# Branch products of a hybrid encoder block: where the tanh pool lies, how early weights are asked for, and at which units the next branch's operands are loaded

## The chip, the core and the metric

The kernel runs on one core of a Trainium2 chip. A core has a matrix engine (PE, with its weight loads shown apart as PEld), three engines for elementwise work (DVE, ACT and POOL) and SP, whose queue issues most of the transfers. Each engine works through its own instructions in order and waits on semaphores where a result of another engine, or a landed transfer, is needed. PE reads its operands from SBUF and writes to PSUM. The metric is the time of one execution on the device in microseconds (us); lower is better.

## The reference, cut to what matters

One encoder block: three mixers (dilated window attention, grouped attention, cross-attention into a memory) give `oa`, `ob` and `om` of 1024 tokens by 512 channels. Each is multiplied by a gate path and projected to 1024 channels; the three products are added under sigmoid gates, and one more projection follows.

```python
ya = (oa * jax.nn.silu(ga)) @ w_br_a[layer]
yb = (ob * jax.nn.silu(gb)) @ w_br_b[layer]
ym = (om * jax.nn.silu(gm)) @ w_br_m[layer]
gates = jax.nn.sigmoid((mg + b_merge[layer]).astype(jnp.float32)).astype(dt).reshape(b, s, N_BRANCHES, d)
merged = gates[:, :, 0] * ya + gates[:, :, 1] * yb + gates[:, :, 2] * ym
out = merged @ w_out[layer]
x = x + rms_norm(out, g_post[layer])
```

The last three lines of gates and products, and `merged`, are the stage that the change edits.

## The kernel before, in words

Everything is computed channels by tokens, in float32 by splitting each operand into a high part in the PE's own format (`hh`, `wh`) and the rest (`hl`, `wl`): a product is three matmul passes, high by high, high by low and low by high. `split` (L104) makes the two parts: ACT copies the high part (L105), DVE subtracts it (L106).

The gates are made first, as tanh, in products that save multiplications by the Strassen scheme (the loop at L1410, seven products a pair, `slot` and `evac`). Their results go to DRAM as `thd`, a tile of 128 channels by 1024 tokens for each of 3 branches and 8 channel blocks. The last ones are written from the tiles `rs` (L1283) by ACT's queue (L1288).

Then come the branch products, 24 units: `steps` (L1336) counts them with m, n is the branch in the order 2, 1, 0 of i, and f the channel block. A unit (`y_unit`, L1444) is 24 matmuls of 512 columns at L125 into a PSUM tile `sc`, of which there are three. For one unit these things are done in other places:

- `y_load(m)` (L1338) asks for its weights (`wbr`, 256 KB) into a raw tile `wr`, of which there are two, so the load for unit m waits until the raw tile of unit m - 2 has been split. `y_split(m)` (L1344) makes the two parts, in a ring of two `wh` tiles.
- `th_load(m)` (L1434) brings its tanh tile (512 KB) back from `thd`, four buffers.
- `y_evac(m)` (L1456) multiplies PSUM by (1 + tanh) on DVE: for the first branch straight into an accumulator `acc` (L1462), later into `th` (L1464), which POOL then adds to `acc` (L1465).

The operands of the next branch are prepared in the same loop, four tiles k = 0 to 3. `g_load(j, k)` (L1312) loads the attention output `ot` and the gate path (into `gt` or into `raw`), 512 KB each, both from DRAM; for branch 1 `r_load(k)` (L1319) adds two row broadcasts `raw<-rld` of 256 KB. One unit later `g_mult` (L1325) multiplies them on DVE (L1327, and L1329 for the broadcast), and one unit after that `g_split` (L1331) splits the product into `hh` and `hl`. From m = 10 on the weights of the last projection are loaded too (`wo_load`, L1440) and from m = 12 on split (DVE writes `wol`, or `hl` once that is free).

From L1237 on the order is written out by hand: ACT, DVE, POOL and SP work in the order of the program, as PE does throughout. So the order of the calls in the loop at L1479 is the order on each engine. What is issued after L1511 (the last projection with `gp`, `xt`, `res`) is placed by a scheduler.

Tiles live in pools that are stacked in SBUF. A tile that lies on a closed pool's memory waits for the last users of what lay there. In the kernel before, `mg` (the last projection's weights and the accumulators) lies at the bottom of the space that the Strassen stage leaves, and `my` (the `th` and `raw` tiles) above it, there on the `ch` and `rs` tiles. A third pool, `pre`, on the other side, has `ot` and `gt`. There are eight completion semaphores for transfers, used in turn, so a transfer also waits until the one eight places earlier has landed.

Of the kernel before, what the change touches and what calls it, by code (L numbers as in the profile page):

```python
# [15 lines left out]
S = 1024  # L16
# [34 lines left out]
def block(ctx: ExitStack, tc: tile.TileContext, x, xT, memT, cst, msk, bcst, tabA, gpost,  # L51
# [21 lines left out]
    def end_psum():  # L73
        bank["pool"].__exit__(None, None, None)
# [29 lines left out]
    def split(dst_h, dst_l, src):  # L104
        A.activation(dst_h, src, AF.Copy)  # L105
        V.tensor_tensor(dst_l, src, dst_h.bitcast(F32), op=OP.subtract)  # L106
# [128 lines left out]
    def pool(name, side="left"):  # L235
        p = tc.tile_pool(name=name, bufs=1, side=side, reuse_waits="tile")
        return p, p.__enter__()

    def close(p):
        p.__exit__(None, None, None)  # L240
# [584 lines left out]
    with tc.tile_pool(name="aa", bufs=1, reuse_waits="tile") as aa:  # L825
# [344 lines left out]
        def load_pair(n, u):  # L1170
            BL[n][u] = wp.tile([P, 1024], F32, name="wr", bufs=WR)
            nc.sync.dma_start(BL[n][u], wu[U_M + pairs[n][u]])

        def own_blocks(n):
            wh = wp.tile([P, 1024], R, name="wh")
            wl = wp.tile([P, 1024], R, name="wl")
            split(wh, wl, BL[n][0])
            for j in range(2):
                BL[n][("A11", "A12")[j]] = wh[:, half[j]], wl[:, half[j]]
# [17 lines left out]
        def split_block(nm, k):  # L1197
            h, l = TB[nm][k]
            split(h, l, l.bitcast(F32))
# [54 lines left out]
    def weight_sum(n, j):  # L1254
        u, v, op = {1: (part(n, 2), part(n, 3), OP.add), 2: (SF[0], part(n, 0), OP.subtract),
                    3: (part(n, 0), part(n, 2), OP.subtract), 4: (part(n, 1), SF[1], OP.subtract)}[j]
        G.tensor_tensor(SF[j - 1], u, v, op=op)  # L1257

    def block_of(n, nm):
        src = part(n, 3) if nm == "A22" else SF[int(nm[1]) - 1]  # L1260
        t = sr.tile([P, 2, 512], R, name="ch", bufs=5)
        split(t[:, 0], t[:, 1], src)
        BL[n][nm] = t[:, 0], t[:, 1]
# [48 lines left out]
    def g_load(i, k):  # L1312
        ot = pre["p"].tile([P, S], F32, name="ot", bufs=4)
        nc.sync.dma_start(ot, od[i, k])
        gt = my.tile([P, S], F32, name="raw", bufs=3) if i < 2 and k % 2 else pre["p"].tile([P, S], F32, name="gt", bufs=1)
        nc.sync.dma_start(gt, g2d[i, k])
        GG[i, k] = [ot, gt]

    def r_load(k):  # L1319
        rt = my.tile([P, S], F32, name="raw", bufs=3)  # L1320
        for h in range(2):
            nc.sync.dma_start(rt[h * 64:h * 64 + 64], rld[2 * k + h:2 * k + h + 1].to_broadcast([64, S]))
        GG[1, k].append(rt)

    def g_mult(i, k):  # L1325
        ot, gt = GG[i, k][:2]
        V.scalar_tensor_tensor(ot, ot, 0.5, gt, op0=OP.mult, op1=OP.mult)  # L1327
        if i == 1:
            V.tensor_tensor(ot, ot, GG[i, k][2], op=OP.mult)  # L1329

    def g_split(i, k, t):  # L1331
        b = k + 4 * (i == 1)
        split(hh[b][:, t], hl[b][:, t], GG[i, k][0][:, t])
# [4 lines left out]
    def y_load(m):  # L1338
        if m < len(steps):
            _, i, f = steps[m]  # L1340
            YW[m] = wp.tile([P, 1024], F32, name="wr", bufs=WR)
            nc.sync.dma_start(YW[m][:, 0:512], wbr[i, f])

    def y_split(m):  # L1344
        if m < len(steps):
            t = wp.tile([P, 1024], R, name="wh")
            split(t[:, 0:512], t[:, 512:1024], YW[m][:, 0:512])
            YW[m] = [t[:, 512 * x:512 * x + 512].rearrange("p (k f) -> p k f", k=4) for x in range(2)]

    pre = {}  # L1350
# [3 lines left out]
    def slot(n, i):  # L1354

        first = n == 0
        if not first and i == 1 and n < last:
            load_pair(n + 1, 1)
        if i == 6 and n + 1 < last:
            load_pair(n + 2, 0)  # L1360
        todo_ = (("S2",), ("S3", "A22"), ("S4",), ("S1",)) if first else (("A22",), ("S4",), ("S1",))
        for nm in todo_[i] if i < len(todo_) else ():
            block_of(n, nm)
        if first:
            for nm, k in {2: (("T1", 0), ("T1", 1)), 3: (("T1", 2), ("T1", 3)), 4: (("T4", 0), ("T4", 1)),
                          5: (("T4", 2), ("T4", 3))}.get(i, ()):
                split_block(nm, k)
        if n < last:
            if i == 3:
                weight_sum(n + 1, 1)  # L1370
                weight_sum(n + 1, 3)
                own_blocks(n + 1)
            elif i == 4:
                weight_sum(n + 1, 2)
                block_of(n + 1, "S3")
            elif i == 5:
                weight_sum(n + 1, 4)
                block_of(n + 1, "S2")
        if (n, i) in COM:
            com[COM[n, i]]()  # L1380
        if (n, i) == (5, 0):
            close(cbp)
            pre["pp"], pre["p"] = pool("pre", "right")
        k = n - (last - 4)
        if 0 <= k < 4:
            if i == 0:
                g_load(2, k)
            elif i == 4:
                g_mult(2, k)
        if n == last:  # L1390
            if i == 0:
                y_load(0)
                y_load(1)
            elif i in (3, 4):
                for k in range(2 * i - 6, 2 * i - 4):
                    g_split(2, k, lo)
            elif i in (5, 6):
                for k in range(2 * i - 10, 2 * i - 8):
                    g_split(2, k, hi)
            if i == 2:  # L1400
                y_split(0)

    for j in (1, 2, 3, 4):
        weight_sum(0, j)
# [19 lines left out]
    phase_psum("ps_o", s2=3)  # L1424


    mgp, mg = pool("mg")
    myp, my = pool("my")
    accs = [None] * 8
    wo = [(hh[k + 4], hl[k + 4]) for k in range(4)]  # L1430
    wo += [(mg.tile([P, D], R, name=f"woh{k}"), mg.tile([P, D], R, name=f"wol{k}")) for k in range(4, 8)]
# [2 lines left out]
    def th_load(m):  # L1434
        if m < len(steps):
            _, i, f = steps[m]
            THS[m] = my.tile([P, S], F32, name="th", bufs=4)
            nc.sync.dma_start(THS[m], thd[8 * i + f])

    def wo_load(k):  # L1440
        raws[k] = my.tile([P, D], F32, name="raw", bufs=3)
        nc.sync.dma_start(raws[k], wout[k])

    def y_unit(m):  # L1444
        n, i, f = steps[m]
        wh, wl = YW.pop(m)
        s = pss()
        for h in half:
            terms = []
            for k in range(4):  # L1450
                gh, gl = [x[k + 4 * (i == 1)][:, h] for x in (hh, hl)]
                terms += [(wh[:, k], gh), (wh[:, k], gl), (wl[:, k], gh)]
            passes(s[:, int(h.start > 0)], terms)
        return s

    def y_evac(m, s):  # L1456
        n, i, f = steps[m]
        sv = s.rearrange("p a b -> p (a b)")
        th = THS.pop(m)
        if n == 0:  # L1460
            accs[f] = mg.tile([P, S], F32, name=f"acc{f}")
            V.scalar_tensor_tensor(accs[f], th, 1.0, sv, op0=OP.add, op1=OP.mult)  # L1462
        else:
            V.scalar_tensor_tensor(th, th, 1.0, sv, op0=OP.add, op1=OP.mult)  # L1464
            (V if m == 23 else G).tensor_tensor(accs[f], accs[f], th, op=OP.add)  # L1465

    def out_operand():
        return wp.tile([P, 8, 128], R, name="wh"), wp.tile([P, 8, 128], R, name="wl")

    def out_split(ah, al, T, k):  # L1470
        src = accs[k][:, T * 128:T * 128 + 128]
        A.activation(ah[:, k], src, AF.Copy, scale=0.5)
        V.scalar_tensor_tensor(al[:, k], src, 0.5, ah[:, k].bitcast(F32), op0=OP.mult, op1=OP.subtract)

    WO = (4, 5, 6, 7, 0, 1, 2, 3)
    th_load(0)
    th_load(1)
    yp = None
    for m, (n, i, f) in enumerate(steps):  # L1479
        s = y_unit(m)  # L1480
        if yp:
            y_evac(*yp)
        yp = m, s
        y_load(m + 2)
        th_load(m + 2)
        if n < 2:
            j = 1 - n
            if f in (0, 1, 3, 5):
                k = (f + 1) // 2
                g_load(j, k)  # L1490
                if j == 1:
                    r_load(k)
        y_split(m + 1)
        if n < 2:
            if f - 1 in (0, 1, 3, 5):
                g_mult(j, f // 2)
            if f - 2 in (0, 1, 3, 5):
                g_split(j, (f - 1) // 2, slice(0, S))
        if m >= 10:
            if m < 18:  # L1500
                wo_load(WO[m - 10])
            if 12 <= m < 20:
                split(*wo[WO[m - 12]], raws[WO[m - 12]])
        if m == 23:
            first = out_operand()
            for k in range(6):
                out_split(*first, 0, k)
# [2 lines left out]
        out_split(*first, 0, k)  # L1510
    manual.__exit__(None, None, None)  # L1511

    close(myp)
    fop, fo = pool("fo")
    gp = fo.tile([P, D], F32, name="gp")
    nc.sync.dma_start(gp, gpost)
    prep = pre["pp"]
    for T in range(NT):
        t = slice(T * 128, T * 128 + 128)
        ah, al = first if T == 0 else out_operand()  # L1520
# [41 lines left out]
                (nc.scalar if h == 1 else nc.sync).dma_start(out[t, c], res[:, c])  # L1562
    close(fop)
    close(mgp)
    close(prep)
    end_psum()


# [118 lines left out]
```

## Time and profile before

| | |
|---|---|
| median of three runs | 1482.71 us (1479.0 to 1483.06) |
| the profiled execution | 1480.33 us |
| its span, first to last instruction | 1478.5 us |
| mean granted PE clock | 0.997 |
| PE, matmuls | 1446.5 us busy, 98% of the span |
| DVE, ACT, POOL | 966.6, 625.3 and 511.8 us busy (65, 42 and 35%) |
| DMA moved | 147.07 MB, mean 99 GB/s |

A row of a timeline has the start in us from the span's start, the length, the engine (a q behind it for the engine's queue of transfers), the line, the operation, what it writes <- what it reads, the sizes and, in brackets, how long the engine had been idle before it and who ended that wait. A row of the chain of waits has start, length and what the end of the program was waiting for in that stretch. PE's busy time says little about its pace, since matmuls overlap; the distance from one start to the next does.

### The profile page before, as it was taken

How to read it: one execution, taken by the hardware profiler on the slowest of the kernel's cores; microseconds unless marked ns; L12 is line 12 of the kernel's file. 1: busy time of each engine (PE TensorE's matmuls, PEld its weight loads, DVE VectorE, ACT ScalarE, POOL GpSimd, SP SyncE). 2: the span in 40 equal slices, each digit the busy share in tenths (PEclk: the TensorE clock that was granted, in tenths of full speed). 3: DMA queues.
4: the chain of work that ended last, by engine and by line, in shares of the span. 5: the costliest groups of instructions: out<-in, count | busy, mean ns of one | idle time of the engine just before them, and what ended most of it. 6: DMA issues, size and time to landing. Idle time of an engine off the chain costs nothing.

```text
span 1478.5 us, 20900 instructions
## 1 busy us (share of the span) xinstructions
PE 1446.5 (98%) x7712; PEld 1160.2 (78%) x7712; DVE 966.6 (65%) x1686; ACT 625.3 (42%) x1404; POOL 511.8 (35%) x400
## 2 busy tenths in 40 slices
PE   7999989999999999999999999999999999899998
PEld 7899976666666888888888888888788888688887
DVE  7755468677773566456655755673888786689443
ACT  6544345565555144344443534454533433222221
POOL 1425424556666332123223312321334330034322
PEclk9999999999999999999999999999999999999999
DMA  6332012222211211112113111332543443986222
GB/s 237 105 106 72 30 47 86 93 93 76 72 61 38 88 43 32 43 45 73 57 44 74 44 44 45 88 100 65 159 143 128 172 171 125 309 284 221 67 97 100
DMA packets 66854, 147.07 MB, mean 99 GB/s; under 512 B 15104, under 2 KB 25024, under 8 KB 66624
## 3 DMA queue, kind: packets, MB, share of 16 engines
q1 hardware_dynamic: 60272, 134.07, 28.3%
q10 hardware_dynamic: 6480, 11.67, 2.2%
q8 instruction: 60, 0.98, 0.3%
q14 instruction: 42, 0.34, 0.1%
HBM read 111.79 MB, written 33.91 MB: 99 GB/s over the span
## 4 chain that ended last, share of the span: by engine, by line
PE 83%; DVE 6%; ACT 3%; POOL 2%; DMA 2%; issue 2%; SPq 0%; POOLq 0%; DVEq 0%; ACTq 0%
PE s L125 14%; PE d L143 12%; PE d L147 12%; PE d L145 12%; PE sc L125 8%; PE sc L1538 5%; PE ov L741 3%; PE tr L1008 3%; PE s L945 2%; PE d L534 2%; PE s L726 1%; PE s L725 1%; PE tr L707 1%; DMA th<-thd 1%; PE tr L991 1%
## 5 line engine op out<-in xcount | busy, mean ns | idle before, releaser
L143 PE MATMUL d<-hh,wh 128*128 128x512 f32 x864 | 345.8, 400 | 1.9 <-DVE fth L222 1.7
L147 PE MATMUL d<-hh,wl 128*128 128x512 f32 x864 | 347.0, 402 | 0.0
L145 PE MATMUL d<-hl,wh 128*128 128x512 f32 x864 | 342.3, 396 | 0.0
L143 PEld LDWEIGHTS d<-hh,wh 128*128 128x128 f32 x864 | 162.9, 189 | 43.4 <-issue 7.7
L147 PEld LDWEIGHTS d<-hh,wl 128*128 128x128 f32 x864 | 162.9, 189 | 36.0 <-issue 5.2
L105 ACT ACTIVATE wh<-wr 128x1024 fp32r<-128x1024 f32 (+1 forms) x89 | 83.8, 943 | 251.2 <-PE d L145 148.3
L145 PEld LDWEIGHTS d<-hl,wh 128*128 128x128 f32 x864 | 162.8, 188 | 34.7 <-issue 4.7
L732 POOL TENSOR_TENSOR bl<-bl,bp 128x512 f32<-128x512 f32 x96 | 130.8, 1362 | 60.8 <-ACT bp L728 55.3
L125 PE MATMUL sc<-hh,wh 128*128 128x512 f32 x384 | 120.3, 394 | 5.6 <-DVE wh L106 3.4
L864 POOL TENSOR_TENSOR aq<-t1a,t2a 128x512 f32<-128x512 f32 x24 | 54.5, 2270 | 163.6 <-DVE t1a L858 163.6
L858 DVE SCALAR_TENSOR_TENSOR t2a<-d,tab 32x512 f32<-32x512 f32 x96 | 66.0, 687 | 63.1 <-PE d L147 62.1
L106 DVE TENSOR_TENSOR wl<-wr,wh 128x1024 fp32r<-128x1024 f32 x65 | 85.7, 1320 | 26.7 <-ACT wh L105 26.7
L864 POOL TENSOR_TENSOR ak<-t1a,t2a 128x512 f32<-128x512 f32 x24 | 55.1, 2296 | 117.5 <-DVE t1a L857 117.5
L708 DVE TENSOR_REDUCE bn<-tr 128x1 f32<-128x512 f32 x128 | 85.4, 684 | 14.9 <-PE tr L707 14.1
L728 ACT ACTIVATE bp<-s 128x512 f32<-128x512 f32 x128 | 75.6, 594 | 46.1 <-PE s L726 43.4
L125 PEld LDWEIGHTS sc<-hh,wh 128*128 128x128 f32 x384 | 72.7, 190 | 22.2 <-DVE wh L106 4.2
L1465 POOL TENSOR_TENSOR acc<-acc,th 128x1024 f32<-128x1024 f32 x15 | 41.2, 2743 | 120.5 <-DVE th L1464 120.5
L857 DVE TENSOR_TENSOR t2a<-d,tab 32x512 f32<-32x512 f32 x96 | 66.0, 687 | 24.9 <-PE d L147 21.2
L1257 POOL TENSOR_TENSOR sf<-wr 128x512 f32<-128x512 f32 x22 | 29.5, 1359 | 140.5 <-DVE ch L106 73.5
L957 DVE CUSTOM_DVE_ANT_0 pra<-s,mask 128x192 f32<-128x192 f32 (+2 forms) x192 | 56.9, 348 | 32.0 <-PE s L945 23.5
L125 PE MATMUL sc<-hl,wh 128*128 128x512 f32 x192 | 75.4, 393 | 0.2 <-DVE hl L106 0.2
L965 ACT ACTIVATE pra<-pra,sts 128x128 f32<-128x128 f32 (+2 forms) x152 | 66.5, 439 | 20.0 <-DVE sts L957 20.0
(317 smaller groups left out, 3126.6 us busy)
## 6 DMA issues: line engine op xcount, KB each, us to landing
wr<-in_wu SPq DMA_DIRECT2D x76, 512.0 KB
th<-thd SPq DMA_DIRECT2D x24, 512.0 KB
thd<-rs ACTq DMA_DIRECT2D x44, 256.0 KB
g2d<-fth SPq DMA_DIRECT2D x24, 256.0 KB
wgt<-wgd SPq DMA_DIRECT2D x24, 256.0 KB
ot<-od SPq DMA_DIRECT2D x12, 512.0 KB
wr<-in_wbr SPq DMA_DIRECT2D x24, 256.0 KB
wr<-in_wmem SPq DMA_DIRECT2D x8, 512.0 KB
```

Of the source, the lines that this page charges most:

```text
L105: A.activation(dst_h, src, AF.Copy)
L106: V.tensor_tensor(dst_l, src, dst_h.bitcast(F32), op=OP.subtract)
L125: PE.matmul(out_ps, a, b, start=i == 0, stop=i == n - 1)
L143: PE.matmul(dst, wh[:, k, :], hh[k][:, t], start=k == 0, stop=False)
L145: PE.matmul(dst, wh[:, k, :], hl[k][:, t], start=False, stop=False)
L147: PE.matmul(dst, wl[:, k, :], hh[k][:, t], start=False, stop=k == 7)
L708: fp["last"] = V.tensor_reduce(st[i]["n"][:, j, c:c + 1], s, axis=AX.X, op=OP.min)
L728: A.activation(pp, s, AF.Exp, scale=-1.0)
L732: G.tensor_tensor(lsum[i % 2], lsum[i % 2], pp, op=OP.add)
L864: G.tensor_tensor(half_of(o, half, g), classes(t1, g), classes(t2, g), op=OP.add)
L965: A.activation(src, raw, AF.Exp, scale=-1.0, bias=bias, accum_out=sts[:, h, 1, T:T + 1])
L1538: PE.matmul(parts[h], *terms[h][j], start=j == 0, stop=j == 23)
```

## The change

Three edits. The pools `my` and `mg` change places: `my`, with the `th` and `raw` tiles, is opened first and lies at the bottom, `mg` above it. They are closed accordingly, so that the tiles of the output stage (`fo`) now lie on the memory of `pre`. In the last pair of the Strassen loop a third weight load, `y_load(2)`, is issued right after `y_split(0)`, and in the loop the load goes from two units ahead to three, behind `y_split(m + 1)` instead of ahead of it. The operands of the next branch are loaded at f = 0, 2, 4 and 5 instead of 0, 1, 3 and 5, multiplied one unit later and split two units later as before, and all of these calls now stand behind `y_split(m + 1)`.

```diff
             if i == 2:
                 y_split(0)
+                y_load(2)
...
+    myp, my = pool("my")
     mgp, mg = pool("mg")
-    myp, my = pool("my")
...
+    AT = (0, 2, 4, 5)
     WO = (4, 5, 6, 7, 0, 1, 2, 3)
...
         yp = m, s
-        y_load(m + 2)
+        y_split(m + 1)
+        y_load(m + 3)
         th_load(m + 2)
         if n < 2:
             j = 1 - n
-            if f in (0, 1, 3, 5):
-                k = (f + 1) // 2
-                g_load(j, k)
+            if f - 1 in AT:
+                g_mult(j, AT.index(f - 1))
+            if f - 2 in AT:
+                g_split(j, AT.index(f - 2), slice(0, S))
+            if f in AT:
+                g_load(j, AT.index(f))
                 if j == 1:
-                    r_load(k)
-        y_split(m + 1)
-        if n < 2:
-            if f - 1 in (0, 1, 3, 5):
-                g_mult(j, f // 2)
-            if f - 2 in (0, 1, 3, 5):
-                g_split(j, (f - 1) // 2, slice(0, S))
+                    r_load(AT.index(f))
...
-    close(myp)
+    close(pre["pp"])
     fop, fo = pool("fo")
...
-    prep = pre["pp"]
...
     close(fop)
     close(mgp)
-    close(prep)
+    close(myp)
```

## The prediction

> **What bounds the kernel now.** I read the page first: PE is busy 98% of the span, so only its gaps can be won or lost. Then the chain of waits, in the part that the edits reach.
>
> ```profile
> 1251.12 1.23 DVE acc L1462
> ...
> 1254.85 9.03 DMA th<-thd
> 1263.88 1.21 DVE acc L1462
> ...
> 1266.09 7.40 DMA th<-thd
> ...
> 1274.27 65.70 PE sc L125 x283
> 1339.97 3.35 DVE hl L106
> ...
> 1343.36 41.57 PE sc L125 x182
> 1384.93 66.58 PE sc L1538 x294
> ```
>
> The 24 branch units (L125, tile sc, 24 matmuls each) lie between 1245.48 and 1384.93. The output product, 66.58 / 294 = 0.2265 us a matmul, runs without a gap, so a unit costs 24 x 0.2265 = 5.44 and 24 units 130.5. The stage takes 139.4: 8.9 us are lost in it, and the chain leaves PE there for DMA and DVE. The PE timeline shows where:
>
> ```profile
> 1263.90 0.50 PE L125 MATMUL sc<-hh,wh 128*128 128x512 f32 x1 [1.94 <-ACT wh L105]
> 1265.74 0.73 PE L125 MATMUL sc<-hh,wh 128*128 128x512 f32 x2 [1.11 <-DVE wh L106]
> ...
> 1271.28 0.50 PE L125 MATMUL sc<-hh,wh 128*128 128x512 f32 x1 [0.26 <-ACT wh L105]
> ...
> 1274.27 1.22 PE L125 MATMUL sc<-hh,wh 128*128 128x512 f32 x2 [2.25 <-DVE wh L106]
> 1275.29 0.63 PE L125 MATMUL sc<-hl,wh 128*128 128x512 f32 x1
> ...
> 1343.36 0.50 PE L125 MATMUL sc<-hl,wh 128*128 128x512 f32 x1 [0.24 <-DVE hl L106]
> ```
>
> The gaps are at units 3 and 4 (split weights late) and once at unit 16 (operand hl late). After 2.25 us the matmuls come 0.43 apart for eight of them, 1.6 us more. The windows name the resource under the first gaps (columns: length, busy time of PE, PEld, DVE, ACT, POOL, granted clock, DMA share, GB/s):
>
> ```profile
> 1251.00:1263.00 12.00, 10.96 (x49) 8.75 (x47) 3.41 (x4) 0.63 (x1) 0.00 (x0) 1.00 0.94 293
> 1263.00:1281.00 18.00, 13.48 (x49) 10.10 (x50) 13.32 (x13) 4.01 (x5) 0.00 (x0) 0.91 1.04 335
> 1341.00:1385.00 44.00, 43.76 (x194) 35.90 (x193) 33.80 (x28) 9.88 (x19) 23.04 (x9) 1.00 0.51 169
> ```
>
> The DMA engines are full from 1251 to 1281. Why everything starts only at 1251, SP's own timeline and its waits tell:
>
> ```profile
> 1240.23 10.79 SPq L1438 DMA_DIRECT2D th<-thd  x2
> 1251.13 0.37 SPq L1342 DMA_DIRECT2D wr<-in_wbr  x1
> 1251.55 0.42 SPq L1438 DMA_DIRECT2D th<-thd  x1
> ...
> 1253.02 1.10 SPq L1322 DMA_DIRECT2D raw<-rld  x2
> 1254.22 0.53 SPq L1342 DMA_DIRECT2D wr<-in_wbr  x1
> ...
> 1265.71 0.33 SPq L1342 DMA_DIRECT2D wr<-in_wbr  x1
> ```
>
> ```profile
> SPq L1438 <- DMA thd<-rs: 10.0, 1, 10.0
> ```
>
> SP stood 10 us before the second th load, whose tile lies on the rs tiles that are being written out; the weights of unit 2 stood behind it. DVE then shows the sequence on which my sum rests:
>
> ```profile
> 1234.02 0.69 DVE L106 TENSOR_TENSOR wh<-wr,wh 128x512 fp32r<-128x512 f32 x1
> ...
> 1250.25 0.69 DVE L106 TENSOR_TENSOR wh<-wr,wh 128x512 fp32r<-128x512 f32 x1 [1.82 <-ACT wh L105]
> ...
> 1260.25 1.23 DVE L1327 SCALAR_TENSOR_TENSOR ot<-ot,gt 128x1024 f32<-128x1024 f32 x1 [4.09 <-DMA gt<-g2d]
> 1262.73 1.22 DVE L1329 TENSOR_TENSOR ot<-ot,raw 128x1024 f32<-128x1024 f32 x1 [1.25 <-DMA raw<-rld]
> 1263.87 1.21 DVE L1462 SCALAR_TENSOR_TENSOR acc<-th,sc 128x1024 f32<-128x1024 f32 x1
> 1265.00 0.68 DVE L106 TENSOR_TENSOR wh<-wr,wh 128x512 fp32r<-128x512 f32 x1
> ...
> 1271.26 1.22 DVE L106 TENSOR_TENSOR hl<-ot,hh 128x1024 fp32r<-128x1024 f32 x1
> ```
>
> DVE is in order: while L1329 waits for its row broadcast, the evacuation of a finished unit and the split of the weights that PE needs next wait behind it.
>
> **The change part by part.** It adds and removes no instruction; both programs have the same count on every engine. What moves:
>
> *The early stall (pool below, y_load(2) in the last slot).* th 0 and 1 no longer lie on rs tiles, so SP's 10.0 us stop goes; unit 2's weights are asked for behind the split of unit 0's (the 1234.02 row), near 1235, and land under the last Strassen products. But the next entry, the weights of unit 3, waits for unit 1's raw buffer (two wr buffers only), freed when the split at 1250.25 ends, 1250.94. That split waits for ACT, which nothing here moves. So SP goes on at 1251.13 as before, with unit 3's weights where unit 2's stood. The stop is traded for another of nearly its length: worth 1254.22 - 1251.13 = 3.1 us to unit 3's weights and nothing to the operands behind them.
>
> *The order in the loop.* y_split now stands ahead of y_load, and the operands behind both. A load three ahead reuses the buffer of the split just made, so it leaves at the same release as the old load two ahead one unit later: no gain. The th, ot, gt and rld loads issued behind it leave one unit later than they did. Queued behind SP's wait are those five; g_mult one unit later waits for them, and behind g_mult on DVE the evacuation and the split of the weights for two units on, which in turn release SP's next group. That closes a loop which the old order did not have: there the group left ahead of the split.
>
> *The price of one turn.* A group is 256 KB of weights, th, ot and gt of 512 KB and two rld of 256 KB, 2.36 MB. In the trace such a group left at 1251.13 and L1329 began at 1262.73: 11.60. That one had a th of 0.52 MB ahead, issued 0.43 earlier; at 293 to 335 GB/s it held the queue 1.57 to 1.79, so without it 10.3. From the start of L1329 to SP's next weight issue: 1265.71 - 1262.73 = 2.98 (L1329, L1462, L106). A turn is 13.28. Two units of PE are 10.88. The bound above is the row itself, 11.60 and 14.58. Below, a lone transfer:
>
> ```profile
> 1247.89 0.33 ACTq L1288 DMA_DIRECT2D thd<-rs  x1
> ```
>
> SP's wait for it ended at 1250.70 (the 10.79 row less its last 0.32), 2.81 after issue; the other 2.10 MB at 335 GB/s take 6.26: 9.07, a turn of 12.05. I take 10.3, the row of the same sequence.
>
> *Units 3 to 8 at f = 0, 2, 4, 5.* The split for unit 3 is done at 1251.13 + 13.28 = 1264.41; PE needs it at its third matmul, 1245.48 + 3 x 5.44 + 0.45 = 1262.25: 2.2 late. The group of f = 2 leaves then, so unit 5's split is done at 1277.69; PE comes there at 1264.41 + 4.98 + 5.44 + 0.45 = 1275.28: 2.4 late. Unit 7 likewise: 1290.97 against 1288.56, 2.4. The group of f = 5 follows at once: its row lands one group (2.36 MB at the mean of 293 and 335, 7.5) after that of f = 4, 1251.13 + 26.56 + 10.3 + 7.5 = 1295.5; then L1329, hl, evacuation and split, 1.14 + 1.13 + 1.14 + 0.68 = 4.1: 1299.6, while unit 8 wants it at 1296.4, 3.2 late. Its other 22 matmuls take 4.98, restart 0.15, and 1.6 for the slow ones that followed the 2.25 gap: unit 9 starts at 1306.35. (After units 5 and 7 slow matmuls cost nothing: the next wait absorbs them.) Before, unit 9 started 118 matmuls after 1274.27: 26.73 + 1.6 = 1302.6. First branch: **+3.75** (by the bounds 9.07 and 11.60, with or without the 1.6: -2.1 to +8.0).
>
> *Units 9 to 16.* With POOL adding, DVE is the tight engine:
>
> ```profile
> 1308.26 1.22 DVE L1464 SCALAR_TENSOR_TENSOR th<-th,sc 128x1024 f32<-128x1024 f32 x1 [0.28 <-PE sc L125]
> ...
> 1319.54 1.21 DVE L1464 SCALAR_TENSOR_TENSOR th<-th,sc 128x1024 f32<-128x1024 f32 x1
> ...
> 1321.27 3.41 DVE L1327 SCALAR_TENSOR_TENSOR ot<-ot,gt 128x1024 f32<-128x1024 f32 x1
> 1324.60 1.22 DVE L106 TENSOR_TENSOR wol<-raw,woh 128x1024 fp32r<-128x1024 f32 x1
> 1325.74 1.21 DVE L1464 SCALAR_TENSOR_TENSOR th<-th,sc 128x1024 f32<-128x1024 f32 x1
> ```
>
> An iteration with two whole-tile operations besides the split takes 1325.74 - 1319.54 = 6.20, over PE's 5.44. From m = 12 to the last operand's split the old positions (1, 2, 4, 6 for g_mult, 2, 3, 5, 7 for g_split) put one such extra in each iteration besides wol; the new ones (1, 3, 5, 6 and 2, 4, 6, 7) put a g_split more into the same four, 1.14 by the hl row. In exchange m = 12 begins without the old backlog, 1319.54 - 1308.26 - 10.88 = 0.40. The wait at unit 16 grows by **+0.74**; bounds: -0.45, the whole old wait with its restart, and +1.14.
>
> *The last branch and the tail.* gp and xt now lie on the closed pre pool and are issued among the last weight loads. Cover: DMA is half idle there (0.51, 169 GB/s); without it, 1.6 us each. PE had no gap in the output product, so nothing is won: 0.
>
> Sum: 3.75 + 0.74 = +4.5. The profiled execution is 1480.33 (span 1478.5 and 1.8 around it), so its like is 1484.8. The median of the three runs stands 2.4 above it; on that, **1487.2**.
>
> *A rule against this sum.* The row: after 2.25 us idle the clock fell (0.91 in that window). The Trainium skill, "TensorE: Matmul & The Clock Gate", under "What's actually happening", says that the clock is halved after at least one whole idle window of about 3.4 us. The trace differs: a shorter gap was enough. By the rule unit 8's 3.2 would cost no slow matmuls and the sum would be 1.6 less, +2.9.
>
> **The rivals.** *A wash.* The group lands at the lower bound: unit 9 starts at 1300.4 to 1302.0, sum -1.4 to +0.2, 1482. For it: transfers here no longer queue behind another group. Against: 9.07 takes the best rate for all of it. *Faster:* the early weights alone decide; if a group landed within 10.88 - 2.98 = 7.9 of its issue, no turn would exceed two units, units 3 to 8 would run through, and 8.6 of the 8.9 would be won less 0.7: 1475. Against: 7.9 lies below even the bound. *Much slower:* 11.60 holds at every turn; units 3, 5, 7 and 8 wait 3.5 to 3.8 each, unit 9 starts at 1310.6, +8.7: 1491.4. For it: it is the measured row. *Not what it says* (weights three ahead) is part of my forecast: with two buffers the third is not sooner.
>
> **How the numbers follow.** Forecast, +3 to +7: 0.50, of which 0.36 above 0.3% (4.4 us, about what a measurement of this kernel can tell from no change). Wash 0.23, much slower 0.16, faster 0.11. So slower 0.16 + 0.36 = 0.52, within 0.14 + 0.23 = 0.37, faster 0.11. The range goes from the middle of the wash to the slow bound, 1481.5 to 1492; faster and a little at the top are left out.
>
> **What would show it.** Right: no stop of SP before the second th load; wr for unit 2 issued near 1235; units 3, 5, 7 and 8 waiting 2 to 3.5 us each for DVE wh, with L1329 waiting for raw<-rld 10 us after its group's weight issue; unit 16 waiting about 1 us for hl. Wrong: no waits at units 5 and 7 (a turn under 10.88), or unit 8 starting before 1292, or a gap in the output product.

## The result, and the profile after

The changed kernel takes 1489.61 us (median of six runs, 1486.51 to 1493.75); six runs of the kernel before, taken beside it, have a median of 1480.7. The ratio is 1.0059, with a 95% interval of 1.004 to 1.0079: slower by 0.6%. The forecast was 1487.2 in a range of 1481.5 to 1492. The profiled execution of the changed kernel is its lowest, 1486.51 with a span of 1484.7, against 1480.33 and 1478.5 before; a second profiled execution, 1488.97 with a span of 1487.2, was taken later. The medians of the experiments leave out three executions far slower than all others, 3721.11 us with the pools alone, 2414.97 with the operands first and 2415.63 with the old units. The lines of the stage stand a few numbers off in the new program: the th load is L1439, the evacuation L1463 and L1465, POOL's addition L1466, the output product L1537.

The chain of waits of the first profile after (start, length, what the end was waiting for):

```profile
1254.84 8.02 DMA raw<-rld
1269.73 8.15 DMA th<-thd
1281.04 6.46 DMA gt<-g2d
1287.52 9.09 DMA raw<-rld
1300.88 43.45 PE sc L125 x190
1346.20 3.34 DVE hl L106
...
1391.14 66.58 PE sc L1537 x294
```

Before, the chain left PE for two landings of the stage's transfers; now it does so for four, in a row. The output product is the same 66.58. It starts 144.1 us after unit 0 (1391.14 - 1247.04, the first start from the PE timeline), 139.45 before (1384.93 - 1245.48): the stage takes 4.65 longer, the forecast's sum being 4.5. The PE timeline of the same execution has six gaps in the stage:

```profile
1265.99 0.72 PE L125 MATMUL sc<-hh,wh 128*128 128x512 f32 x2 [2.02 <-DVE wh L106]
...
1279.74 0.74 PE L125 MATMUL sc<-hh,wh 128*128 128x512 f32 x2 [0.97 <-DVE wh L106]
...
1292.93 0.74 PE L125 MATMUL sc<-hh,wh 128*128 128x512 f32 x2 [1.98 <-DVE wh L106]
...
1300.88 0.73 PE L125 MATMUL sc<-hh,wh 128*128 128x512 f32 x2 [0.54 <-DVE wh L106]
...
1346.26 0.74 PE L125 MATMUL sc<-hh,wh 128*128 128x512 f32 x2 [1.50 <-DVE wh L106]
...
1349.59 0.50 PE L125 MATMUL sc<-hl,wh 128*128 128x512 f32 x1 [1.20 <-DVE hl L106]
```

They are at units 3, 5, 7, 8 and twice at unit 16; the old ones were at units 3 and 4 and once at 16. SP's timeline and then DVE's show the loop that the prediction drew:

```profile
1239.08 2.11 SPq L1439 DMA_DIRECT2D th<-thd  x2
1252.53 0.33 SPq L1342 DMA_DIRECT2D wr<-in_wbr  x1
...
1265.96 0.33 SPq L1342 DMA_DIRECT2D wr<-in_wbr  x1
...
1279.71 0.33 SPq L1342 DMA_DIRECT2D wr<-in_wbr  x1
...
1292.91 0.34 SPq L1342 DMA_DIRECT2D wr<-in_wbr  x1
```

```profile
1262.98 1.23 DVE L1329 TENSOR_TENSOR ot<-ot,raw 128x1024 f32<-128x1024 f32 x1 [1.32 <-DMA raw<-rld]
1264.12 1.21 DVE L1463 SCALAR_TENSOR_TENSOR acc<-th,sc 128x1024 f32<-128x1024 f32 x1
1265.25 0.69 DVE L106 TENSOR_TENSOR wh<-wr,wh 128x512 fp32r<-128x512 f32 x1
...
1276.73 1.23 DVE L1329 TENSOR_TENSOR ot<-ot,raw 128x1024 f32<-128x1024 f32 x1 [0.87 <-DMA raw<-rld]
...
1289.92 1.22 DVE L1329 TENSOR_TENSOR ot<-ot,raw 128x1024 f32<-128x1024 f32 x1 [1.10 <-DMA raw<-rld]
```

The 10 us stop before the second th load is gone (both th loads leave within 2.11 us), and SP stands instead until 1252.53 before the weights of unit 3. From there a group leaves, its row lands 10.45 later, DVE multiplies, evacuates and splits, and at the end of that split SP sends the next: turns of 13.43, 13.75 and 13.20 us, where PE needs 10.88 for the two units that a turn must feed. The second profile has the same loop with less even landings:

```profile
1265.69 0.73 PE L125 MATMUL sc<-hh,wh 128*128 128x512 f32 x2 [1.31 <-DVE wh L106]
1281.05 1.22 PE L125 MATMUL sc<-hh,wh 128*128 128x512 f32 x2 [4.18 <-DVE wh L106]
1294.77 0.73 PE L125 MATMUL sc<-hh,wh 128*128 128x512 f32 x2 [1.12 <-DVE wh L106]
1303.07 0.74 PE L125 MATMUL sc<-hh,wh 128*128 128x512 f32 x2 [2.55 <-DVE wh L106]
```

Same units, other sizes. Its stage takes 146.17 (unit 0 at 1247.45, output product at 1393.62), 6.72 more than before.

Between the first profiles, 1.56 us of the difference lie ahead of the stage (unit 0 at 1247.04 against 1245.48), and whether the change makes them had to be tried; the last experiment answers it.

### The profile page after: what moved, and what is told of

It is laid out like the page before. It is cut to its first block, busy times and chain, and to the rows that moved or that the text cites. A ratio compares the mean times of both kernels' runs of the same rounds, so it can differ in the third digit from the quotient of the medians.

```text
span 1484.7 us, 20894 instructions
## 1 busy us (share of the span) xinstructions
PE 1450.4 (98%) x7712; PEld 1162.3 (78%) x7712; DVE 958.3 (65%) x1686; ACT 625.6 (42%) x1404; POOL 512.0 (34%) x400
## 4 chain that ended last, share of the span: by engine, by line
PE 83%; DVE 6%; DMA 3%; ACT 2%; issue 2%; POOL 2%; SPq 1%; POOLq 0%; DVEq 0%; ACTq 0%
PE s L125 14%; PE d L143 12%; PE d L147 12%; PE d L145 12%; PE sc L125 6%; PE sc L1537 4%; PE ov L741 4%; PE tr L1008 3%; PE s L945 2%; PE s L726 2%; PE s L725 2%; PE d L534 2%; PE tr L707 2%; DMA raw<-rld 1%; PE tr L991 1%
## 5 line engine op out<-in xcount | busy, mean ns | idle before, releaser
L1466 POOL TENSOR_TENSOR acc<-acc,th 128x1024 f32<-128x1024 f32 x15 | 41.1, 2737 | 125.3 <-DVE th L1465 125.3
```

## The experiments

Each time is a median and stands beside runs of the kernel before taken with it (medians 1481.38, 1480.22 and 1481.55 in three groups).

**The pools alone.** The kernel before, with nothing but the pools exchanged (and closed accordingly).

```diff
-    mgp, mg = pool("mg")
     myp, my = pool("my")
+    mgp, mg = pool("mg")
...
```

> The kernel before with the two pools exchanged and nothing else. My theory (the changed order of the calls made the loss: operand loads behind the split, whose wait on DVE they in turn prolong): SP's 10.0 us stop before the second th load goes, the first operand group is asked for near 1242 instead of 1252 and lies ready, the gaps at units 3 and 4 (8.6 us with their slow matmuls) go: 7 to 9 us under the kernel before. Rival (the lower th tiles themselves cost the time, by new waits or collisions): slower than before by 4 us or more.

> The kernel before with the pools alone exchanged, for the rows of its trace. Theory (SP's 10 us stop is gone, and the first group leaves behind unit 2's weights, near 1240): L1329 of the first operand starts before 1252, no gap of over 0.5 us at units 3 and 4, 0.2 to 0.3 at unit 16, the 24 units take 131 to 132.5 us. Rival (the gain comes from elsewhere, the output stage): the units take 137 us or more and the 66.58 of the output product shrink.

Measured: 1474.54 us, ratio 0.995 [0.9936, 0.9964]; in the second entry, a single execution, 1473.08. SP's timeline of the latter:

```profile
1238.46 1.91 SPq L1438 DMA_DIRECT2D th<-thd  x2
1240.47 0.38 SPq L1342 DMA_DIRECT2D wr<-in_wbr  x1
...
1243.24 0.32 SPq L1314 DMA_DIRECT2D ot<-od  x1
...
1248.76 1.10 SPq L1322 DMA_DIRECT2D raw<-rld  x2
1251.93 0.34 SPq L1342 DMA_DIRECT2D wr<-in_wbr  x1
```

The first group of operands is out before the weights of unit 3, the entry that must wait for unit 1's split. So the row product comes early enough; the only gap of PE in the whole stage is the old one at unit 16:

```profile
1336.14 0.50 PE L125 MATMUL sc<-hl,wh 128*128 128x512 f32 x1 [0.24 <-DVE hl L106]
```

L1329 of the first operand started at 1255.89, later than the 1252 that was expected, and still in time. The stage takes 131.26 (1246.43 to 1377.69), the 66.58 of the output product stay. One edit of the three, alone, wins 8.2 of the 8.9 us that the kernel before lost in the stage.

**Everything but the pools.** The changed kernel with the pools as before.

```diff
-    myp, my = pool("my")
     mgp, mg = pool("mg")
+    myp, my = pool("my")
...
```

> The changed kernel with the pools left as they were: order of the calls, weights three ahead, new units. My theory: SP is held by unit 1's split until the same moment anyway, so the pools are worth nothing to this order: within 2 us of the changed kernel, gaps at units 3, 5, 7 or 8, and 16. Rival (the pools make the loss): as fast as the kernel before, within 2 us.

Measured: 1490.47, ratio 1.0062 [1.0048, 1.0076], within 1 us of the changed kernel. SP's timeline:

```profile
1240.95 11.12 SPq L1439 DMA_DIRECT2D th<-thd  x2
1252.16 0.38 SPq L1342 DMA_DIRECT2D wr<-in_wbr  x1
```

The stop of some 10 us between the two th loads is back, and the first group leaves at 1252.16 instead of 1252.53. In the changed order the two stops end together, so taking away one is worth nothing. That is the trade that the prediction named.

**The operands first.** The changed kernel, with the loads of the operands ahead of the next split and so ahead of the weights three units on.

```diff
+        j = 1 - n
+        if n < 2 and f in AT:
+            g_load(j, AT.index(f))
+            if j == 1:
+                r_load(AT.index(f))
         y_split(m + 1)
         y_load(m + 3)
...
-            if f in AT:
-                g_load(j, AT.index(f))
-                if j == 1:
-                    r_load(AT.index(f))
```

> The changed kernel with one thing moved: the loads of the next branch's operands stand ahead of y_split again; weights three ahead, pools and units 0, 2, 4, 5 stay. My theory: the loop of 13.4 us is broken, no gaps at units 3, 5, 7 and 8, about 1 us at unit 16 (the later units of the operands): 13 to 16 us under the changed kernel, 6 to 9 under the one before. Rival (weights three ahead or the later units make the loss): within 3 us of the changed kernel.

Measured: 1474.1, ratio 0.9945 [0.9932, 0.9958], 15.5 under the changed kernel, 7.3 under the one before. Its PE timeline has one gap in the stage:

```profile
1337.22 0.50 PE L125 MATMUL sc<-hl,wh 128*128 128x512 f32 x1 [0.98 <-DVE hl L106]
```

The move is one of place in SP's queue only: DVE's and ACT's order stay.

**Two units ahead.** The changed order of calls, the weights at the old distance.

```diff
-                y_load(2)
...
-        y_load(m + 3)
+        y_load(m + 2)
```

> The changed kernel with the weights asked for two units ahead as before, but still behind the split of the next unit, with the operands still last: only the distance of the weight load is undone. SP's order of transfers is then that of the kernel before, while the place of the calls is that of the changed one. Theory (the distance makes the loss, through the raw tile that is not free): no gap at units 3 to 8 above 0.5 us, 1473 to 1477 us. Rival (the operands' place behind the split makes it): like the changed kernel, 1486 to 1492.

Measured: 1475.19, ratio 0.9965 [0.9953, 0.9977]. No gap at units 3 to 7, one of 1.51 at unit 8 (above the 0.5 that was expected), 0.97 at unit 16. So it is not the operands' place behind the split that costs, but the entry that they stand behind: a load that asks for a tile not yet free.

**Four raw buffers.** The order of the changed kernel, but the weight load finds a free place.

```diff
-            YW[m] = wp.tile([P, 1024], F32, name="wr", bufs=WR)
-            nc.sync.dma_start(YW[m][:, 0:512], wbr[i, f])
+            if m < 2:
+                YB[m] = wp.tile([P, 1024], F32, name="wr", bufs=WR)
+            YW[m] = YB[m % 2][:, 512 * (m // 2 % 2):512 * (m // 2 % 2) + 512]
+            nc.sync.dma_start(YW[m], wbr[i, f])
...
```

> The changed kernel, order of all calls as it is, but the raw weights of branch products lie in the four halves of the two raw tiles in turn (one half of each stood empty), so that a load three units ahead never waits for a split that is still to come. Theory (the loss is SP standing before a weight load whose raw tile is not free, with the operands behind it): units 3 to 8 run without a gap, SP never stops before a weight load there for more than about a unit, and the time is 1473 to 1476 us, as with the operands first. Rival (the loss comes from the amount of data that is asked for together, or from the place of the split in DVE's order, which both stay): gaps at units 3, 5, 7 and 8 remain, 1484 us or more.

Measured: 1474.63, ratio 0.9962 [0.995, 0.9974]. SP's timeline:

```profile
1238.87 0.80 SPq L1442 DMA_DIRECT2D th<-thd  x2
1239.72 0.42 SPq L1345 DMA_DIRECT2D wr<-in_wbr  x1
...
1243.64 0.32 SPq L1314 DMA_DIRECT2D ot<-od  x1
```

The weights of unit 3 leave at 1239.72, 12.8 us sooner than in the changed kernel. The group behind them follows in pieces, `ot` at 1243.64 and the row at 1248.64, which is still 5.7 us sooner. Nothing is moved in the order; the loss is gone. Gaps: 0.10 at unit 8, 0.98 at unit 16.

**Without the row product.** This kernel leaves out the loads of the row broadcast and the product by it, so branch 1 lacks a factor.

```diff
-        if i == 1:
-            V.tensor_tensor(ot, ot, GG[i, k][2], op=OP.mult)
...
-                if j == 1:
-                    r_load(AT.index(f))
```

> The changed kernel without the row broadcasts raw<-rld of branch 1 and without the product by them (L1329 left out, so branch 1's operand lacks its factor by row). A turn of SP's loop then has 1.84 MB in place of 2.36 and ends with L1327, which started 7.9 us after the weight issue in the changed kernel, and 2.98 for L1327, the evacuation and the split: 10.9, about the two units of PE (10.88). Theory (the length of a turn against two units sets the waits): unit 3 waits under 0.7 us, units 5, 7 and 8 under 0.5, no slow matmuls, the first branch takes 52.5 to 53.5 from the start of unit 0 to that of unit 9 less the 49.0 of its matmuls and what is left of gaps, so 49.0 to 50.5 us against 58.98; the time is 1479 to 1483 us. Rival (SP's stop before the weights costs by itself, whatever the group's size): turns stay above 12.5 us, gaps of 1 us or more at units 5 and 7, 1486 or more.

Measured: 1475.04, ratio 0.9965 [0.9952, 0.9978]. DVE's timeline, the four products that are left:

```profile
1259.50 1.23 DVE L1327 SCALAR_TENSOR_TENSOR ot<-ot,gt 128x1024 f32<-128x1024 f32 x1 [5.33 <-DMA gt<-g2d]
...
1270.42 1.23 DVE L1327 SCALAR_TENSOR_TENSOR ot<-ot,raw 128x1024 f32<-128x1024 f32 x1 [5.10 <-DMA raw<-g2d]
...
1281.29 1.23 DVE L1327 SCALAR_TENSOR_TENSOR ot<-ot,gt 128x1024 f32<-128x1024 f32 x1 [5.04 <-DMA gt<-g2d]
```

DVE still stands 5 us before each, so SP's loop is still there; but its turns are 10.92 and 10.87, PE's own two units, and units 3 to 8 run without a gap. The stop costs nothing so long as a turn is no longer than the work that it feeds. The time came out 4 us under the expected range. That range had taken the first branch of the first profile (58.98 us from unit 0 to unit 9, against 48.96 here) for the usual one; in the second profile it is 62.36, 13.4 more than here. The units behind it gain about 1 us too.

**The old units.** First in the changed order, then with the operands first.

```diff
-    AT = (0, 2, 4, 5)
+    AT = (0, 1, 3, 5)
```

> The changed kernel with the operands at units 0, 1, 3, 5 as before; order, lead and pools as changed. My theory: the loop stays and only its units move, gaps of 2 to 4 us at units 3, 4 and 8: within 3 us of the changed kernel. Rival (the later units make the loss): back to the kernel before, 5 to 9 us under the changed one.

> The changed kernel with the next branch's operands asked for ahead of the weights three units on, as in the run with the operands first, and at the old units f = 0, 1, 3 and 5. Theory (the later units are worth nothing in themselves and cost the longer wait at unit 16, 0.98 us in the run with the operands first against 0.24 in the kernel before): the wait at unit 16 falls to 0.2 to 0.5, no gap at units 3 to 8, 1473.0 to 1474.0 us, 0.3 to 0.9 under the run with the operands first. Rival (the later units keep the queue free where the old ones did not): gaps of 0.5 us or more come back at unit 3 or 4, and the time is 1475 or above.

Measured: in the changed order 1487.8, ratio 1.0048 [1.0031, 1.0064], within 2 us of the changed kernel; the gaps of the first branch only sit at units 3, 4, 6 and 8. With the operands first 1473.45, ratio 0.9961 [0.9948, 0.9975], and in the PE timeline:

```profile
1336.40 0.50 PE L125 MATMUL sc<-hl,wh 128*128 128x512 f32 x1 [0.25 <-DVE hl L106]
```

0.98 becomes 0.25. The later units cost 0.73 at unit 16 (the stage falls from 132.00 to 131.27), and nothing else is seen of them. This version has the lowest median; the pools alone (1474.54) have the same 131.3 us stage.

**The operands first, on the old pools.** The edit of the operands first and that of the pools put back, together.

> The run with the operands first (weights three ahead, units 0, 2, 4 and 5), but the pools as in the kernel before. SP then stands before the second th load until about 1251.1 again, and the first group of operands leaves right behind it. Theory (the pools are what lets the operands of the first turn leave early, once nothing else holds them; afterwards no turn is late): L1329 of the first operand starts near 1261 to 1261.5, the split of unit 3 is done 2.98 later, some 1.0 to 2.0 us too late, no other gap up to unit 8, 0.98 at unit 16; 1474.5 to 1477.5 us. Rival (without the pools nothing is won): gaps of 4 us or more in units 3 to 8, 1479 or more. Second rival (the pools are worth nothing once the operands are first): no gap at unit 3, 1474.1 as with them.

Measured: 1478.0, ratio 0.9978 [0.9969, 0.9987]. The PE timeline up to unit 8:

```profile
1264.48 0.74 PE L125 MATMUL sc<-hh,wh 128*128 128x512 f32 x2 [0.77 <-DVE wh L106]
...
1293.88 0.74 PE L125 MATMUL sc<-hh,wh 128*128 128x512 f32 x2 [1.91 <-DVE wh L106]
```

L1329 came at 1261.47, as expected, and unit 3 waited 0.77, a little less than the 1.0 to 2.0 that were expected. The 1.91 at unit 8 was not expected, and with it the time lies 0.5 above its range; like the 1.51 of the weights two ahead it follows a late last operand (L1329 of the fourth at 1289.74 and 1288.78, against 1286.30 with the operands first on the new pools). Why that one lands later was not tried. The pools are worth 3.9 us here, nothing in the changed order, and 6.8 alone.

**The changed kernel once more.**

> The changed kernel once more, for what makes its runs differ by up to 7 us. Theory (the turns are the same in each run, 13.2 to 13.8 us, and how many half-clock stretches of 1.6 us follow the gaps differs): the turns are within 0.4 us of the first profile's, and the number of stretches at half clock among units 3 to 8 moves with the run's time, 1.6 us each. Rival (the landing of the groups differs): the turns differ by 1 us or more.

Measured: 1488.97, the second profile shown above. The turns are 12.72, 15.37 and 13.72, the first 0.7 shorter, the second 1.6 and the third 0.5 longer than in the first profile, with two stretches of slow matmuls in each profile. So the landing differs between executions, as the rival said; the theory that slow stretches alone make the spread falls. L1329 of the second group started 12.38 after its weight issue (1278.04 - 1265.66), against 10.77 in the first profile.

**The kernel before once more.**

> The kernel before once more, for where its stage starts. In its first profile unit 0 starts at 1245.48, in all profiles of changed programs at 1246.20 to 1247.45, though nothing ahead of the stage is edited but one weight load. Theory (the difference is that of one execution from the next): unit 0 starts at 1246 to 1247.5, and the stage from unit 0 to the output product again takes 138.5 to 140.5 us. Rival (the edits make what comes ahead of the stage longer by some 1 to 2 us): unit 0 starts at 1245.2 to 1245.8.

Measured: 1482.4 (span 1480.6). Unit 0 starts at 1247.23 and the output product at 1387.05, so the stage takes 139.82, as in the first profile (139.45), and the early start of that one belongs to its execution. Its PE timeline has the old gaps at units 3 and 4, in other sizes:

```profile
1266.93 0.79 PE L125 MATMUL sc<-hh,wh 128*128 128x512 f32 x1 [3.22 <-ACT wh L105]
...
1268.87 1.22 PE L125 MATMUL sc<-hh,wh 128*128 128x512 f32 x2 [0.71 <-DVE wh L106]
...
1277.87 0.73 PE L125 MATMUL sc<-hh,wh 128*128 128x512 f32 x2 [1.51 <-DVE wh L106]
```

## Why the prediction was right, and where it was not

*The direction and the place.* The forecast rested on the loop from group to split to group, and that is what both profiles show. The stage, whose sum the prediction made (+4.5), takes 144.10 and 146.17 in the two profiles of the changed kernel, 139.45 and 139.82 in the two of the kernel before: +5.5 between the means. That the first profile's 4.65 lies beside the sum is luck: its first branch lost 1.9 less than the term for it, the units behind it 2.1 more. Between the medians it is +8.9, double the sum and outside the +3 to +7. By size that is the rival "much slower" (+8.7), but its reason, a landing of 11.60 at every turn, stands in neither profile. The time itself came nearer (1487.2 against 1489.61) because the sum was put on 1482.71, the median of three runs of the kernel before, where that of the six is 1480.7. The first profile of the changed kernel is its fastest run, the second 0.6 under its median; what the slower executions lose beyond these two was not seen in a trace. Only their mean granted clock is on record, 0.992 and 0.991 in the two slowest against 0.994 in the fastest, which hints at more slow matmuls and shows no cause.

*The early stall.* Right: SP's stop went and another ended at the same place, which the run without the pools shows (1490.47). What the prediction did not say is that it is the longer distance that puts the second stop ahead of the operands: with the weights two ahead the first group leaves before that stop, and the pools alone are worth 6.8 us.

*The order in the loop.* Right, and now narrower. The load three ahead is no sooner with two raw tiles, as forecast, and it is the one entry that blocks those behind it. A free buffer, the old distance or the operands ahead of it each take 14 to 15.5 us off.

*The price of a turn.* 13.28 predicted; 13.43, 13.75 and 13.20 in the first profile, 12.72, 15.37 and 13.72 in the second. The landing of 10.3 measured 10.45, 10.77, 10.21, then 9.74, 12.38 and 10.73: within the bounds of 9.07 and 11.60 five times in six. The wash would have needed the lower bound at each turn. That a turn within two units would cost nothing was the reason of the rival "faster", at 1475: the run without the row product has turns of two units, and 1475.04.

*Units 3 to 8.* The predicted ends of the splits, moved by the later start of unit 0 (1.56), are 1265.97, 1279.25, 1292.53 and 1301.2 at units 3, 5, 7 and 8; PE went on at 1265.99, 1279.74, 1292.93 and 1300.88. What differs is the share of the slow matmuls. The prediction put one slow stretch behind unit 8, where nothing absorbs it. In the first profile the stretches came after units 3 and 7, and the waits at 5 and 8 took them in, so that units 0 to 8 took 58.98 us: +1.85 on the 57.13 before, not +3.75. In the second profile one came after unit 8, and it is 62.36: +5.23. The mean of the two, +3.5, is near the term; the single sizes are not, and two profiles make no sure mean. The prediction's sign, waits of 2 to 3.5 us at each of the four units, held less well than the ends of the splits: of the eight waits in the two profiles two lie in it (2.02 and 2.55), one is longer (4.18) and five are shorter, since PE came later behind slow matmuls or the group landed sooner.

*Units 9 to 16.* Here a step failed: "m = 12 begins without the old backlog". It does not. DVE's timeline of the first profile after, in the second branch:

```profile
1312.62 1.22 DVE L1327 SCALAR_TENSOR_TENSOR ot<-ot,gt 128x1024 f32<-128x1024 f32 x1 [4.58 <-DMA gt<-g2d]
...
1323.16 1.23 DVE L1327 SCALAR_TENSOR_TENSOR ot<-ot,raw 128x1024 f32<-128x1024 f32 x1 [2.51 <-DMA raw<-g2d]
1324.30 1.21 DVE L1465 SCALAR_TENSOR_TENSOR th<-th,sc 128x1024 f32<-128x1024 f32 x1
...
1340.75 1.45 DVE L1327 SCALAR_TENSOR_TENSOR ot<-ot,raw 128x1024 f32<-128x1024 f32 x1 [1.90 <-DMA raw<-g2d]
```

The operands of the third branch come late for the same reason as those of the second: SP sends their groups right behind weights, at 1315.61 and 1326.14, which leave when the splits of wh on DVE end (1315.58 and 1326.12). There, without the row, DVE stands 1.90 to 4.58 us before each operand, in a stretch in which it has no slack. In m = 12 the evacuation starts at 1324.30, 2.0 after the unit (1322.34), and so the weights and the low part of unit 16 are late together. Units 9 to 23 take 2.8 us more than before in the first profile and 1.5 in the second, instead of 0.74. The run without the row product, where the first branch loses nothing and this loop stays, still waits 0.45 and 1.24 at unit 16; with the operands first or four raw buffers only the 0.98 is left. The 0.74 itself, for the later units, is what the two runs with the operands first differ by, 0.73. The prediction worked out the loop for the first branch and left it out of the second.

*The last branch and the tail.* Right: no gap in the output product, 66.58 as before.

*The rule against the sum.* The rule of the Trainium skill ("TensorE: Matmul & The Clock Gate", "What's actually happening") would have had no slow matmuls behind gaps under 3.4 us. The first profile has two such stretches, behind 2.02 and 1.98, and its window says so (length, busy time of PE, PEld, DVE, ACT and POOL, granted clock, DMA share, GB/s):

```profile
1266.00:1300.00 34.00, 31.05 (x120) 24.56 (x120) 18.53 (x18) 5.52 (x8) 0.00 (x0) 0.90 0.81 255
```

The sum was right to count slow matmuls behind such gaps; at which gap they come it could not know (last section).

## What to carry to other kernels

In an in-order queue a load that must wait for its buffer holds all that is issued behind it, so a prefetch distance greater than the number of buffers turns a weight load into a barrier; count the buffers before lengthening the distance, and put the loads that have room ahead of the one that has none. A closed loop of load, use and next load costs nothing until its turn is longer than the work that it feeds, and then its excess at every turn: work out that one number, and do it for every loop through which the same order runs. An edit that is worth nothing in one order (the pools) may be worth nearly the whole gain in another, so the parts of a change are to be measured alone.

## What the runs showed of the hardware

The slow matmuls follow some gaps and not others. Across the profiles taken, stretches of some six to eleven matmuls about 0.43 us apart stood behind gaps of 1.98 to 4.42 us, and none behind 1.94 (the kernel before, unit 3), 1.91 (the operands first on the old pools) and 1.71 (everything but the pools); one gap of 3.02, in the changed order with the old units, had none either. So the length of the gap alone does not decide it. Its place does, in these profiles: the stretches of granted clock 0.5 in this stage are 3.41 us long, or twice that, and within one profile they start a whole number of steps of 3.413 us apart (1266.95 and 1294.26 in the first profile after, eight steps). Cut PE's rows into these steps: of the steps at full clock, each with 1.91 to 3.41 us idle had such a stretch right behind it (2.02 and 1.98 in the first profile after), and none with 1.87 or less had. The gap of 3.02 is cut by the edge of a step at 1289.82 into 1.87 and 1.15. No run moved a gap against the steps by intent, so this is what the profiles agree in and no more.

DVE and POOL disturb each other in the second branch. DVE's rows of the changed kernel, and then POOL's:

```profile
1326.03 3.42 DVE L106 TENSOR_TENSOR hl<-ot,hh 128x1024 fp32r<-128x1024 f32 x1
...
1342.12 1.21 DVE L106 TENSOR_TENSOR hl<-ot,hh 128x1024 fp32r<-128x1024 f32 x1
...
1346.13 3.41 DVE L106 TENSOR_TENSOR hl<-ot,hh 128x1024 fp32r<-128x1024 f32 x1
```

```profile
1325.59 2.78 POOL L1466 TENSOR_TENSOR acc<-acc,th 128x1024 f32<-128x1024 f32 x1 [2.69 <-DVE th L1465]
...
1345.68 2.77 POOL L1466 TENSOR_TENSOR acc<-acc,th 128x1024 f32<-128x1024 f32 x1 [4.57 <-DVE th L1465]
```

The same subtraction takes 1.21 us where no addition of POOL runs (1342.12; the next begins at 1345.68) and 3.42 where an addition of POOL has begun before it: it ends at 1329.45, 1.08 after POOL's end at 1328.37, as if it had only begun then. The Trainium skill, "SBUF — State Buffer" under "SBUF: two separate sides", says that DVE operations with two SBUF inputs and POOL's share a pair of ports, which the first to start holds for its whole instruction; the rows agree. The wait of unit 16 for hl in the last rows is of this kind: the split ran 3.41 instead of 1.21.
